# Two orders in a hybrid encoder kernel: the seventh product's jobs of the gate pair in a row, and token sums no longer tied behind operands

## The chip, the cores and the metric

The kernel runs on one core of a Trainium2 chip. The metric is the device time of one execution in microseconds (us). Its engines are called as the profile calls them: PE is TensorE (PEld its weight loads), DVE is VectorE, ACT is ScalarE, POOL is GpSimd and SP is SyncE. SP and POOL issue the transfers of this kernel, each on a queue of its own.

## The reference

Two layers of an encoder trunk over 512 tokens of width 2048, in float32. Each layer normalises its input, projects it once onto the columns of two head groups, and adds the normalised output projection back:

```
h = rmsnorm(x, g_pre)
z = h @ w_in                                   # 2048 x 7184, split into the columns below
gq, gk, gv, gg, ga, aq, ak, av, ag = split_columns(z)
log_a = log_sigmoid(ga @ w_alpha + b_alpha) / 16
o_gla = rmsnorm(gla_chunk_causal(gq, gk, gv, log_a), g_gla) * silu(gg)
o_att = rmsnorm(chunk_band_attention(aq, ak, av, rel_bias), g_att) * silu(ag)
y = concatenate([o_gla, o_att]) @ w_out
return x + rmsnorm(y, g_post)
```

The first group is a gated linear attention with 4 heads and a state that runs over chunks of 64 frames; the second is attention with 8 heads over a band of chunks. `ag` is the attention group's gate, `ga` the 16 columns from which the forget gate is made.

## The kernel before

**Precision.** Every large product is made of float32 numbers that are split into a high and a low part (`split`, L107): ACT casts the high part (`wh` for a weight, L236), DVE subtracts it from the source to get the low part (`wl`, L246), and PE adds three products, high by high, high by low and low by high.

**Fast products.** A projection block is 512 columns wide. Most are taken in pairs, and a pair is computed by `fast_gemm` with the seven products of a Strassen scheme in place of eight: `P1` to `P7` are products of a sum of weight tiles with a sum of token tiles, and each is cut into four chunks `c` of the inner dimension. One such piece is a `Job`. A job's weight comes from a tile of the ring `H` (four buffers of 512 KB), which holds one weight of the pair, is filled for `P1`, and is then added to or subtracted from for `P5`, `P6`, `P7` and `P4`, and of the ring `raw` (five buffers), which brings the second weight of a sum. DVE makes these sums (L230, L232, L252). The token sums `S1` to `S4` (`LEFT` names which product reads which) are made once per layer by `make_sums`, split, and mostly written to DRAM by POOL (L619); SP brings them back into the ring `sa` (four buffers, L215).

**Jobs and look-ahead.** All jobs of both layers stand in one list, `stream`. When PE has taken a job, `ahead` writes the loads of up to five jobs further and the casts and subtractions of up to four. The order in which a pair's jobs come is a line of text: `"10 50 11 ..."` means `P1` chunk 0, `P5` chunk 0, `P1` chunk 1 and so on. From the program so written a scheduler sets the order of the instructions on each engine; each engine then runs its own in that order. `tc.issue_after(x)` tells the scheduler to place an instruction behind `x`.

**First layer.** The attention gate's columns are not computed as a fast pair but as three plain products (`std_gemm`, blocks AG0, AG1 and AG2; AG1 and AG2 are 264 columns wide, with the gate's tail and `ga` in AG2). During AG0 and AG1 `first_operands` makes the token operands, chunk by chunk; the last instruction of each is kept in the list `ends`. The float32 tokens that the sums are made of stand in `full`, and those of the first half, `full[0, c]`, in the four buffers of the ring `H`. During AG1 and AG2 the task `token_sums` makes the 16 sums from them: per chunk two subtractions `S1` and `S3` (`sub`), then `S2` (L631) and `S4` (L634), each followed by its split. After AG2 comes the first fast pair, AV (attention values), whose `H` loads need the buffers of `full[0, c]`.

**Second layer.** Here AG1 and AG2 form a fast pair of their own (`GATE_PAIR`), in the order `PROD_GATE`. Its weights are 264 wide (264 KB a load), its `P4` takes `H` after the weight of `P2` has been added to it (L252) and loads nothing, and its last read of an `H` buffer is `P4`'s. `P2` is collected in two PSUM tiles of its own (`ax` in the profile). After the pair come the QK products (L430, features on the partitions), whose first job, `P1` chunk 0, loads an `H`. At the end of the gate pair ACT also has the Silu of the gates (L784) and loads another table of functions (L62).

Of the kernel before, what the change touches and what calls it, by code (L numbers as in the profile page):

```python
# [11 lines left out]
ALU = mybir.AluOpType  # L12
# [24 lines left out]
def hybrid_trunk(  # L37
# [13 lines left out]
    nc = tc.nc  # L51
# [20 lines left out]
    def slot(tag, shape, dtype=F32):  # L72
        return slots.tile([P] + shape, dtype, tag=tag, name=nm(tag))
# [19 lines left out]
    def dram(shape, name):  # L93
        return dpool.tile(shape, F32, tag=name, name=name)
# [3 lines left out]
    sa_d = [{(n, c): dram([P, 1024], f"{n}{l}{c}") for n in ("S1", "S2", "S3", "S4", "A22") for c in range(4)} for l in range(L)]  # L98
# [5 lines left out]
    def flat(t):  # L104
        return t.bitcast(F32).rearrange("p a b -> p (a b)")
# [30 lines left out]
    def order(text):  # L136
        return [("P" + z[0], int(z[1])) for z in text.split()]
# [3 lines left out]
    PROD_OUT = order("10 20 11 21 12 13 50 51 60 61 22 23 52 53 62 63 30 31 32 33 70 71 72 73 40 41 42 43")  # L141
    PROD_FRONT = order("20 21 22 23 10 11 12 13")
    PROD_REST = order("50 51 52 53 60 61 30 62 63 31 70 32 71 72 73 33 40 41 42 43")
    PROD_GATE = order("10 50 11 51 12 52 13 53 60 30 61 31 62 32 63 33 70 20 71 21 72 22 73 23 40 41 42 43")
    GATE_PAIR = (AG1, AG2)
    LEFT = {"P5": "S1", "P6": "S2", "P3": "S4", "P7": "S3", "P4": "A22"}
    SPARE = ("g12", "g13", "g16", "g17")
# [107 lines left out]
    for l in range(L):  # L255
        if l:
# [5 lines left out]
            pr = {}  # L262
            stream += [Job(l, k, c, *GATE_PAIR, pr) for k, c in PROD_GATE]
        else:
# [277 lines left out]
    full = {}  # L542
# [57 lines left out]
            A[kh, half, c] = op  # L600
            yield

    def make_sums(dst, tags, parts, home={}, behind=None):
        stage = [0]

        def sub(c, out, a, b):
            with tc.issue_after(behind(c)) if behind and c else nullcontext():
                nc.vector.tensor_tensor(out=out, in0=a, in1=b, op=ALU.subtract)

        def put(name, c, src):  # L610
            if (name, c) in home:
                op = A[name, c] = slot(home[name, c], [2, 512], F32R)
            else:
                tag = tags[stage[0] % len(tags)]
                op = rtile(tag, dtype=F32R) if tag == "H" else slot(tag, [2, 512], F32R)
                stage[0] += 1
            with tc.issue_after(last_cast[0]):
                split(op[:, 0, :], op[:, 1, :], src)
            nc.gpsimd.dma_start(dst[name, c], flat(op))  # L619
            written.add((id(dst), name, c))  # L620

        for c in range(4):
            a11, a12, a21, a22 = parts(c)
            yield
            sub(c, a22, a21, a22)
            put("S1", c, a22)
            yield
            sub(c, a21, a11, a21)
            put("S3", c, a21)
            yield  # L630
            nc.vector.tensor_tensor(out=a22, in0=a22, in1=a11, op=ALU.subtract)  # L631
            put("S2", c, a22)
            yield
            nc.vector.tensor_tensor(out=a12, in0=a12, in1=a22, op=ALU.add)  # L634
            put("S4", c, a12)
            yield

    def token_sums(l):
        tags, home = (("g10", "g16", "H"), HOMES) if l else (STAGE, HOME)
        return make_sums(sa_d[l], tags, lambda c: (full[0, c][:, 0, :], full[0, c][:, 1, :], full[1, c][:, 0, :], full[1, c][:, 1, :]), home, None if l else lambda c: ends[-3 if c == 1 else -1])  # L640

    VT = ("g16", "g17", "g4", "g5", "g6", "g7", "g12", "g13")
    V, U = {}, {}
# [55 lines left out]
            nc.tensor.matmul(ps[:, t * P : (t + 1) * P], ones, dg[:, t, :], start=True, stop=True)  # L699
        nc.scalar.copy(rb, ps)  # L700

    ends = []

    def first_operands():
        for ch in CO:
            kh, c = divmod(ch, 4)
            while ch not in U:
                yield
            for half in range(2):
                if kh == 0:  # L710
                    full[half, c] = rtile("H") if half == 0 else slot(KEEP[c], [2, 512])
                dst = full[half, c][:, kh, :]
                tok = slice(half * 256, (half + 1) * 256)
                with tc.issue_after(ends[-2]) if len(ends) >= 2 else nullcontext():
                    for kk in range(2):
                        nc.vector.scalar_tensor_tensor(
                            out=dst[:, kk * 256 : (kk + 1) * 256], in0=V[ch][:, kk, tok],
                            scalar=gcol[:, 2 * ch + kk : 2 * ch + kk + 1], in1=rb[:, tok], op0=ALU.mult, op1=ALU.mult,
                        )
                if half == 0:  # L720
                    op = slot(f"a1{kh + 1}{c}", [2, 512], F32R)
                elif kh == 0:
                    op = slot(A21[c], [2, 512], F32R)
                else:
                    while cursor[0] < NCH:
                        yield
                    op = rtile("sa", (2, 512), F32R)
                ends.append(split(op[:, 0, :], op[:, 1, :], dst))
                if half and kh:
                    nc.gpsimd.dma_start(sa_d[0]["A22", c], flat(op))  # L730
                A[kh, half, c] = op
                yield
        yield from load_forget_gate(0)
# [43 lines left out]
    def layer(l):  # L777
# [136 lines left out]
        if l:  # L914
# [8 lines left out]
            drain()  # L923
            fast_gemm(l, GATE_PAIR, gate_consume, prod=PROD_GATE)
            tasks.append(load_forget_gate(l))
# [662 lines left out]
```

## Time and profile before

| | us |
|---|---|
| runs (3) | 1615.96, 1617.78, 1618.01; median 1617.78 |
| the profiled execution | 1617.69 |
| its span, from the first to the last instruction | 1615.9 |
| PE busy in it | 1595.7 |
| DVE, ACT, POOL busy | 1279.2, 920.6, 134.9 |
| moved by DMA | 441.39 MB, mean 273 GB/s |

In the profile's rows a group or an instruction is named by its line, engine and operation, and by the tiles it writes and reads, without buffer numbers. In brackets or behind a bar stands how long its engine was idle before it and what ended that. PEclk, or the granted clock, is the share of its full speed that PE's clock had. `q1` is SP's queue of transfers and `q0` POOL's. `SPq` rows are SP issuing a transfer; the transfer itself lands later.

### The profile page before, as it was taken

Reading aid. Unit: us, or ns where it says so; the run is one execution under the profiler, and the core shown is the slowest. Engines: PE = TensorE matmul, PEld = TensorE weight load, DVE = VectorE, ACT = ScalarE, POOL = GpSimd, SP = SyncE. Lnnn points to the kernel's source line nnn. Section 1 sums busy time; section 2 is a strip of 40 time slices with the busy share of each in tenths; the row PEclk is TensorE's granted clock in tenths of the full one; section 3 lists DMA queues with packets and bytes.
Section 4 is the critical chain, followed back from the end, with each engine's and each line's share of the span. In section 5 each row is a group of like instructions: output and inputs, shape, how many; then the busy total and the mean of one; then the engine's idle time right before and its main releaser. Section 6 shows DMA issues by size and latency. Waiting matters only on the chain.

```text
span 1615.9 us, 25135 instructions
## 1 busy us (share of the span) xinstructions
PE 1595.7 (99%) x9158; PEld 1377.2 (85%) x9158; DVE 1279.2 (79%) x1697; ACT 920.6 (57%) x1535; POOL 134.9 (8%) x206
## 2 busy tenths in 40 slices
PE   9989999999999999999999998999999999999998
PEld 7978999998888777888888898999988877788886
DVE  5977868678677877998989877785886878689887
ACT  7545445657455556664786445456575545565654
POOL 0220000000000010100122000000000100101001
PEclk9999999999999999999999999999999999999999
DMA  9797777685767768689889987857858687686887
GB/s 349 234 402 249 260 263 245 215 295 184 269 222 272 273 216 312 223 303 401 299 267 357 364 285 264 308 199 239 312 203 285 216 290 250 218 306 241 330 304 202
DMA packets 137229, 441.39 MB, mean 273 GB/s; under 512 B 14885, under 2 KB 27429, under 8 KB 137073
## 3 DMA queue, kind: packets, MB, share of 16 engines
q1 hardware_dynamic: 119952, 377.86, 66.7%
q0 software_dynamic: 16864, 61.63, 10.9%
q8 instruction: 72, 1.18, 0.3%
q14 instruction: 53, 0.43, 0.1%
q10 hardware_dynamic: 288, 0.30, 0.1%
HBM read 380.20 MB, written 61.62 MB: 273 GB/s over the span
## 4 chain that ended last, share of the span: by engine, by line
PE 87%; DMA 4%; issue 4%; DVE 3%; ACT 1%; POOL 1%; POOLq 0%; SPq 0%; DVEq 0%; ACTq 0%
PE mm L440 51%; PE mm L430 19%; PE mm L353 5%; PE ax L440 3%; PE ax L1009 2%; DMA H<-in_w_dram 2%; DMA raw<-in_w_dram 2%; PE ax L1195 1%; DVE wl L246 1%; PE ax L992 1%; PE ax L1167 1%; PE ax L972 1%; PE ax L971 1%; PE ax L970 1%; DMA S<-g 0%
## 5 line engine op out<-in xcount | busy, mean ns | idle before, releaser
L440 PE MATMUL mm<-wh,sa 128*128 128x512 f32 (+1 forms) x1600 | 510.3, 390 | 1.7 <-DMA sa<-S 1.1
L236 ACT CAST wh<-H 128x1024 fp32r<-128x1024 f32 (+1 forms) x256 | 261.4, 1024 | 213.5 <-PE mm L440 81.7
L246 DVE TENSOR_TENSOR wl<-H,wh 128x1024 fp32r<-128x1024 f32 (+1 forms) x256 | 303.4, 1188 | 92.1 <-PE mm L440 29.4
L440 PEld LDWEIGHTS mm<-wh,sa 128*128 128x128 f32 x1600 | 297.7, 188 | 71.3 <-issue 7.7
L236 ACT CAST wh<-raw 128x1024 fp32r<-128x1024 f32 (+2 forms) x237 | 236.2, 1002 | 202.4 <-PE mm L440 78.2
L246 DVE TENSOR_TENSOR wl<-raw,wh 128x1024 fp32r<-128x1024 f32 (+2 forms) x237 | 272.7, 1154 | 59.8 <-PE mm L440 23.9
L440 PE MATMUL mm<-wl,sa 128*128 128x512 f32 (+1 forms) x800 | 309.3, 387 | 0.0
L430 PE MATMUL mm<-sa,wh 128*128 128x256 f32 x1280 | 237.7, 285 | 0.0
L440 PE MATMUL mm<-wh,a 128*128 128x512 f32 (+1 forms) x672 | 219.1, 391 | 4.1 <-ACT wh L236 4.1
L430 PEld LDWEIGHTS mm<-sa,wh 128*128 128x128 f32 x1280 | 200.4, 191 | 0.4
L430 PE MATMUL mm<-sa,wl 128*128 128x256 f32 x640 | 181.1, 283 | 0.2 <-DVE wl L246 0.2
L440 PEld LDWEIGHTS mm<-wl,sa 128*128 128x128 f32 x800 | 150.3, 188 | 29.2 <-DVE wl L246 0.9
L230 DVE TENSOR_TENSOR H<-H,raw 128x1024 f32<-128x1024 f32 (+1 forms) x144 | 170.1, 1188 | 0.9
L440 PEld LDWEIGHTS mm<-wh,a 128*128 128x128 f32 x672 | 125.1, 189 | 30.0 <-ACT wh L236 5.0
L440 PE MATMUL mm<-wl,a 128*128 128x512 f32 (+1 forms) x336 | 130.8, 390 | 0.0
L430 PEld LDWEIGHTS mm<-sa,wl 128*128 128x128 f32 x640 | 122.4, 191 | 0.5 <-DVE wl L246 0.5
L440 PE MATMUL mm<-wh,g 128*128 128x512 f32 (+1 forms) x416 | 120.5, 368 | 0.5 <-ACT wh L236 0.4
L484 POOL TENSOR_TENSOR sm<-sm,mhalf 128x2 f32<-128x2 f32 (+2 forms) x40 | 50.7, 1267 | 696.6 <-DVE sm L1019 389.4
L232 DVE TENSOR_TENSOR raw<-H,raw 128x1024 f32<-128x1024 f32 (+1 forms) x56 | 66.4, 1186 | 49.7 <-DMA raw<-in_w_dram 45.9
L430 PE MATMUL mm<-a,wh 128*128 128x256 f32 x512 | 96.1, 288 | 3.9 <-ACT wh L236 3.9
L390 ACT COPY ev<-mm 128x512 f32<-128x512 f32 (+1 forms) x112 | 64.2, 573 | 54.8 <-PE mm L440 39.2
L252 DVE TENSOR_TENSOR H<-H,raw 128x1024 f32<-128x1024 f32 (+1 forms) x48 | 56.6, 1180 | 43.8 <-DMA raw<-in_w_dram 42.9
(273 smaller groups left out, 2414.5 us busy)
## 6 DMA issues: line engine op xcount, KB each, us to landing
raw<-in_w_dram SPq DMA_DIRECT2D x287, 512.0 KB, 5.2
sa<-S SPq DMA_DIRECT2D x188, 512.0 KB, 4.4
H<-in_w_dram SPq DMA_DIRECT2D x60, 512.0 KB, 5.6
sa<-A SPq DMA_DIRECT2D x48, 512.0 KB, 5.8
sa<-oS SPq DMA_DIRECT2D x32, 512.0 KB, 5.6
S<-g POOLq DMA_DIRECT2D x30, 512.0 KB, 8.0
raw<-in_w_ag_dram SPq DMA_DIRECT2D x32, 264.0 KB, 4.3
oS<-g POOLq DMA_DIRECT2D x16, 512.0 KB, 4.6
```

Of the source, the lines that this page charges most:

```text
L230: nc.vector.tensor_tensor(out=h, in0=h, in1=r, op=ALU.add)
L232: nc.vector.tensor_tensor(out=r, in0=h, in1=r, op=ALU.subtract)
L236: last_cast[0] = nc.scalar.copy(self.wh[:, z, :], src[:, z, :]).ins
L246: last_low[0] = nc.vector.tensor_tensor(out=self.wl[:, z, :], in0=self.src[:, z, :], in1=self.wh[:, z, :].bitcast(F32), op=ALU.subtract).ins
L252: nc.vector.tensor_tensor(out=h, in0=h, in1=self.src, op=ALU.add)
L353: nc.tensor.matmul(pss[o], a(part, kk, o) if callable(a) else a[:, part, t], rhs[:, kk, :], start=(i == 0 and kk == 0 and m == 0), stop=(i ...
L390: last_copy[0] = nc.scalar.copy(e, src[t]).ins
L430: nc.tensor.matmul(dst, lhs[:, kk, f], a[:, part, tok], start=(fresh and kk == 0 and m == 0 and ft % 2 == 0), stop=(c == 3 and kk == 1 and ...
L440: last_mm[0] = nc.tensor.matmul(out_ps[t], a[:, part, tok], rhs[:, kk, :], start=(fresh and kk == 0 and m == 0), stop=(c == 3 and kk == 1 ...
L484: nc.gpsimd.tensor_tensor(out=out_r, in0=v, in1=mhalf[:, : v.shape[-1]], op=ALU.pow)
L970: nc.tensor.matmul(ps[:, :n], self.qh[:, t], self.kh[:, :n], start=True, stop=False)
L1009: nc.tensor.matmul(o, self.pt[i][:, j * P : (j + 1) * P], av[hd // 4, j // 2][:, j % 2, (hd % 4) * P : (hd % 4 + 1) * P], start=(j == 0), ...
```

## The change

Two things are changed. In the second layer's gate pair the seventh product's four jobs come in a row, and then the second and the last product alternate, chunk by chunk; before, the seventh and the second alternated, and the last product's four jobs came at the end. And in the first layer the subtractions for `S1` and `S3` of chunks 1 to 3 are no longer tied behind the splits that end the operands; what is left of the diff takes the argument for that tie away.

```diff
-    PROD_GATE = order("10 50 11 51 12 52 13 53 60 30 61 31 62 32 63 33 70 20 71 21 72 22 73 23 40 41 42 43")
+    PROD_GATE = order("10 50 11 51 12 52 13 53 60 30 61 31 62 32 63 33 70 71 72 73 20 40 21 41 22 42 23 43")
...
-    def make_sums(dst, tags, parts, home={}, behind=None):
+    def make_sums(dst, tags, parts, home={}):
         stage = [0]
 
-        def sub(c, out, a, b):
-            with tc.issue_after(behind(c)) if behind and c else nullcontext():
-                nc.vector.tensor_tensor(out=out, in0=a, in1=b, op=ALU.subtract)
+        def sub(out, a, b):
+            nc.vector.tensor_tensor(out=out, in0=a, in1=b, op=ALU.subtract)
...
-            sub(c, a22, a21, a22)
+            sub(a22, a21, a22)
             put("S1", c, a22)
             yield
-            sub(c, a21, a11, a21)
+            sub(a21, a11, a21)
             put("S3", c, a21)
...
-        return make_sums(sa_d[l], tags, lambda c: (full[0, c][:, 0, :], full[0, c][:, 1, :], full[1, c][:, 0, :], full[1, c][:, 1, :]), home, None if l else lambda c: ends[-3 if c == 1 else -1])
+        return make_sums(sa_d[l], tags, lambda c: (full[0, c][:, 0, :], full[0, c][:, 1, :], full[1, c][:, 0, :], full[1, c][:, 1, :]), home)
...
-    ends = []
-
     def first_operands():
+        ends = []
```

What the scheduler makes of it is seen on the queues. On SP, between the last loads of AG2 and the first products of AV in the first layer, `H_1154`, `H_1184`, `H_1291` and `H_1325` are the four `H` loads of AV, `raw_1064` to `raw_1124` the last weights of AG2, the other `raw` the second weights of AV, and `sa` its token sums. The transfers in the order before:

```order
L172 DMA H_1154<-in_w_dram 128x1024
L215 DMA sa_1383<-S_86 128x1024
L172 DMA raw_1214<-in_w_dram 128x1024
L172 DMA raw_1295<-in_w_dram 128x1024
L172 DMA raw_1343<-in_w_dram 128x1024
L172 DMA H_1184<-in_w_dram 128x1024
L172 DMA raw_1362<-in_w_dram 128x1024
L172 DMA raw_1381<-in_w_dram 128x1024
L172 DMA H_1291<-in_w_dram 128x1024
L172 DMA raw_1411<-in_w_dram 128x1024
L215 DMA sa_1413<-S_87 128x1024
L215 DMA sa_1432<-S_94 128x1024
```

Behind these comes `H_1325`. In the change the same place reads:

```order
L164 DMA raw_1124<-in_w_ag_dram 128x528
L172 DMA H_1184<-in_w_dram 128x1024
L215 DMA sa_1383<-S_86 128x1024
L172 DMA raw_1214<-in_w_dram 128x1024
L172 DMA raw_1295<-in_w_dram 128x1024
L172 DMA raw_1343<-in_w_dram 128x1024
L172 DMA H_1291<-in_w_dram 128x1024
L172 DMA raw_1362<-in_w_dram 128x1024
L172 DMA raw_1381<-in_w_dram 128x1024
L172 DMA H_1325<-in_w_dram 128x1024
L215 DMA sa_1413<-S_87 128x1024
L215 DMA sa_1432<-S_94 128x1024
```

`H_1154` has moved ahead of AG2's last weight, `H_1184` past four transfers, `H_1291` past two loads counted from the first `H`, and `H_1325` past the three that now stand behind it. On DVE, a little earlier in the same stage, `a_127` and `a_130` are token operands of the first half, `wl` the low parts of AG1's and AG2's weights, and the `g` and `H` tiles those of the sums. Before:

```order
L246 TENSOR_TENSOR wl_864<-raw_776,wh_816 128x528
L109 TENSOR_TENSOR g_129_752<-g_128_749,g_129_752 128x512
L716 SCALAR_TENSOR_TENSOR g_128_749<-g_76_432,gcol,bias_178 128x256 x2
L608 TENSOR_TENSOR g_110_643<-g_110_643 128x512
L631 TENSOR_TENSOR g_67_383<-g_67_383,H_339 128x512
L246 TENSOR_TENSOR wl_909<-raw_818,wh_866 128x528
L109 TENSOR_TENSOR a_130_763<-H_737,a_130_763 128x512
```

In the change (line numbers behind the edit are one or two lower):

```order
L607 TENSOR_TENSOR g_119_696<-g_119_696 128x512
L109 TENSOR_TENSOR g_148_888<-g_110_643,g_148_888 128x512
L630 TENSOR_TENSOR g_67_383<-g_67_383,H_339 128x512
L109 TENSOR_TENSOR g_129_752<-g_128_749,g_129_752 128x512
L714 SCALAR_TENSOR_TENSOR g_128_749<-g_76_432,gcol,bias_178 128x256 x2
L246 TENSOR_TENSOR wl_909<-raw_818,wh_866 128x528
L607 TENSOR_TENSOR g_119_696<-H_684,g_119_696 128x512
L109 TENSOR_TENSOR a_130_763<-H_737,a_130_763 128x512
```

Counted over the whole queue, four instructions of the sums more stand ahead of `a_130_763`: three of those above (`g_119_696` twice, `g_148_888`) and the second subtraction of chunk 1. On SP in the second layer, between the gate pair's last loads and the QK pair, `H_9826` is the first `H` of QK, `H_9852` (`H_9844` in the change) its second. Before:

```order
L164 DMA raw_9725<-in_w_ag_dram 128x528
L215 DMA sa_9872<-S_102 128x1024
L172 DMA raw_9870<-in_w_dram 128x1024
L172 DMA raw_9909<-in_w_dram 128x1024
L215 DMA sa_9911<-S_103 128x1024
L172 DMA raw_9997<-in_w_dram 128x1024
L172 DMA raw_10039<-in_w_dram 128x1024
L215 DMA sa_9999<-S_104 128x1024
L172 DMA raw_10072<-in_w_dram 128x1024
L172 DMA H_9826<-in_w_dram 128x1024
L215 DMA sa_10041<-S_105 128x1024
L172 DMA H_9852<-in_w_dram 128x1024
```

In the change:

```order
L164 DMA raw_9791<-in_w_ag_dram 128x528
L215 DMA sa_9864<-S_102 128x1024
L215 DMA sa_9911<-S_103 128x1024
L172 DMA raw_9862<-in_w_dram 128x1024
L172 DMA raw_9909<-in_w_dram 128x1024
L215 DMA sa_9999<-S_104 128x1024
L172 DMA H_9826<-in_w_dram 128x1024
L215 DMA sa_10041<-S_105 128x1024
L172 DMA raw_9997<-in_w_dram 128x1024
L172 DMA H_9844<-in_w_dram 128x1024
L172 DMA raw_10039<-in_w_dram 128x1024
L172 DMA H_9883<-in_w_dram 128x1024
```

The first `H` has moved up past three loads; the second stands as many transfers behind the last gate weight as the first did, and behind it loads and `H` alternate. On all engines the order differs at these two places alone, from the tail of AG1 to the middle of AV in the first layer and from the gate pair's last third into the QK pair in the second.

## The prediction

> **What bounds the kernel now.** I read the page's first rows, then the waits of TensorE (PE), its timeline at the longest of them, the chain of waits there, and last the clock.
>
> ```profile
> span 1615.9 us, 25135 instructions
> PE 1595.7 (99%) x9158; PEld 1377.2 (85%) x9158; DVE 1279.2 (79%) x1697; ACT 920.6 (57%) x1535; POOL 134.9 (8%) x206
> ```
>
> PE is busy all but 20 us of the span. No instruction is added or removed on it by this change, so it can only win or lose idle time and clock. The waits of PE over the whole span, and behind them the one row that the stretch 60 to 124 us gives for the same wait:
>
> ```profile
> PE mm L440 <- ACT wh L236: 5.1, 6, 3.3
> PE mm L430 <- ACT wh L236: 3.9, 1, 3.9
> ...
> PE mm L440 <- ACT wh L236: 4.5, 4, 3.3
> ```
>
> Two places hold most of it. In PE's timeline (start, duration, what ran, and in brackets the idle time before it):
>
> ```profile
> 73.77 0.39 PE L353 MATMUL mm<-wh,a 128*128 128x264 f32 x1 [0.64 <-ACT t L784]
> ...
> 108.17 0.73 PE L440 MATMUL mm<-wh,a 128*128 128x512 f32 x2 [0.81 <-ACT wh L236]
> ...
> 114.01 0.39 PE L440 MATMUL mm<-wh,g 128*128 128x512 f32 x1
> 117.70 0.73 PE L440 MATMUL mm<-wh,a 128*128 128x512 f32 x2 [3.30 <-ACT wh L236]
> ...
> 976.72 0.28 PE L440 MATMUL mm<-wh,g 128*128 128x264 f32 x1
> 980.91 0.74 PE L430 MATMUL mm<-a,wh 128*128 128x256 f32 x4 [3.92 <-ACT wh L236]
> 982.17 0.58 PE L430 MATMUL mm<-a,wl 128*128 128x256 f32 x1 [0.52 <-DVE wl L246]
> ```
>
> Place A is the start of the first layer's AV pair, place B the start of the second layer's first QK pair. At both, PE waits for the high part `wh` of a weight that stands in a tile `H`, and ACT, which casts it, waits for the load. The chain of waits says so:
>
> ```profile
> 98.52 17.98 DMA H<-in_w_dram
> 118.65 63.98 PE mm L440 x274
> ...
> 969.17 10.56 DMA H<-in_w_dram
> ```
>
> Behind each stall the clock is down. Columns: the stretch, its length, busy time (and count) of PE, PEld, DVE, ACT and POOL, granted clock, DMA share, GB/s; the first row has PE alone.
>
> ```profile
> 70.00:80.00 10.00, 9.36 (x77) 1.00 0.84 277
> ...
> 118.60:122.06 3.46, 3.41 (x8) 2.74 (x9) 3.46 (x4) 0.78 (x1) 0.00 (x0) 0.51 0.53 217
> 982.00:985.60 3.60, 3.43 (x16) 3.43 (x17) 2.86 (x4) 2.59 (x3) 0.00 (x0) 0.53 1.01 396
> ```
>
> So each of the two costs its idle time and about 3.46 x 0.49 = 1.7 us (3.60 x 0.47 = 1.7 us) of lost clock. A: 4.5 + 1.7 = 6.2 us. B: 3.92 + 0.52 + 1.7 = 6.1 us. Together 12.3 us is the most that this change can win there. Around the 0.64 us wait the clock stays at 1.00, so I cost a stall near 1 us at its own length. The Trainium skill (TensorE: Matmul & The Clock Gate, Part 1: The HAM clock gate) gives the half clock after an idle window of about 3.4 us and the full one after a busy window as long. The length agrees; the idle time before 117.70 was only 3.30 us, so going by the page A would have kept its clock, and 1.7 us less would be there to win.
>
> **Place A: the token sums untied.** The four `H` buffers hold the first layer's token chunks until that chunk's last sum is split, and only then can SP load AV weights into them. Untied, the sums stand earlier on DVE, so the loads stand earlier on SP. The fourth `H` had three 512 KB transfers (0.524 MB) ahead of it that now come behind it, and the third had two more loads ahead (the order pieces show both). How fast SP's queue moved between 88 and 118 us, beside POOL's writes of the sums, and the issues at the fourth `H`:
>
> ```profile
> q1 hardware_dynamic: 1785, 6.51, 53.1%
> q0 software_dynamic: 1707, 5.99, 49.1%
> ...
> 90.86 0.78 SPq L172 DMA_DIRECT2D H<-in_w_dram  x1
> 95.38 0.33 SPq L172 DMA_DIRECT2D raw<-in_w_dram  x1
> 95.81 2.52 SPq L215 DMA_DIRECT2D sa<-S  x2
> 98.52 1.08 SPq L172 DMA_DIRECT2D H<-in_w_dram  x1
> ...
> 116.60 1.99 ACT L236 CAST wh<-H 128x1024 fp32r<-128x1024 f32 x2 [7.54 <-DMA H<-in_w_dram]
> ```
>
> SP's queue (q1) got 6.51 MB / 30 us = 0.217 MB/us. Three transfers fewer are 3 x 0.524 / 0.217 = 7.2 us: the load lands at 109.3 instead of 116.5, its cast (1.0 us) ends at 110.3. PE came to the end of its earlier work at 114.4, of which 1.0 us were waits of the same kind (0.81 and, of the 0.4 left of 4.5, one of two). Without those it is there at 113.4. The stall goes, with 3 us in hand. If the whole 12.5 MB of both queues were SP's rate (0.417), the gain in landing is 3.8 us and the cast ends at 113.7, a stall of 0.3 us at most. Two transfers fewer take the wait for the third `H` away on both bounds (4.8 or 2.5 us against 0.8). The Trainium skill (DMA: Bandwidth & Descriptors, Queues, rings and completion order) has each DMA engine go round-robin between queues with work; the two rows, 53% and 49%, agree, and by that rule it is the 7.2 us. What comes late next are the three transfers put back (landing near 116.5). They feed the pair's sixth and third products, three jobs after the fourth `H` is used. A job there is 12 matmuls, 2.8 us by the chain's 63.98 for 274; 8.4 us less an addition and a cast leaves over 5.
>
> The price is on DVE. Ahead of the low part of the last operand of chunk 3 (`a`) stand four more 512-wide sum instructions.
>
> ```profile
> 56.58 0.71 DVE L246 TENSOR_TENSOR wl<-raw,wh 128x528 fp32r<-128x528 f32 x1 [0.37 <-ACT a L108]
> ...
> 70.65 0.69 DVE L109 TENSOR_TENSOR a<-H,a 128x512 fp32r<-128x512 f32 x1
> 71.25 0.68 DVE L608 TENSOR_TENSOR g<-H,g 128x512 f32<-128x512 f32 x1
> ...
> 72.00 0.40 PE L353 MATMUL mm<-wh,a 128*128 128x264 f32 x2
> ```
>
> Start to start one takes 0.60 us, four 2.4. The first of them falls into the 0.37 us in which DVE idled. The low part is then done at 71.34 + 2.4 - 0.37 = 73.37, and PE reads it at 72.00: 1.4 us of stall. The 0.64 us wait behind it, for the eviction of that product, comes later by the same and shrinks a little, since ACT had two casts in front of the eviction and now has had time for them: minus 0.2. I take 1.2 us; bounds 0 (PE finds other matmuls in the new order) and 2.4 (nothing is covered). Place A then wins 6.2 - 1.2 = 5.0 us.
>
> **Place B: the gate pair's order.** Same weights, same operands, same matmuls. The fourth product reads `H` last, and it now stands at jobs 22, 24, 26 and 28 of 28 instead of 25 to 28, so the first `H` frees three jobs earlier, the second two, the third one. In SP's order the first `H` of the QK pair moves up past three 512 KB loads, and the second takes the very place where the first stood. The queue between 966 and 980 us, the cast and what ACT does around it:
>
> ```profile
> q1 hardware_dynamic: 1364, 4.97, 90.2%
> q0 software_dynamic: 221, 0.59, 10.6%
> ...
> 972.14 0.76 ACT L784 ACTIVATE t<-ev 128x264 f32<-128x264 f32 x2 [0.16 <-DVE ev L395]
> ...
> 977.12 0.67 ACT L784 ACTIVATE t<-mm 128x264 f32<-128x264 f32 x2
> 977.81 1.28 ACT L62 ACT_TABLE_LOAD   x1
> 979.82 1.04 ACT L236 CAST wh<-H 128x1024 fp32r<-128x1024 f32 x1 [0.72 <-DMA H<-in_w_dram]
> ...
> 251.30 2.88 PE mm L430 x24
> ```
>
> At 4.97 MB / 14 us = 0.355 MB/us three transfers are 4.4 us: the first `H` lands at 979.7 - 4.4 = 975.3, its cast ends at 976.4, before PE is through the gates at 977.0. With POOL's bytes counted in (0.397) it is 4.0 us and 976.8, just in time. The second `H` lands where the first did, at 979.7, is cast by 980.8 and wanted when the first QK job (24 matmuls, 2.9 us) ends at 979.9. That leaves a stall of 1.0 us. ACT says the same from its side: two more Silus of the second product (0.76 us) and the table load now stand behind the first cast, and 977.12 + 0.67 + 0.76 + 1.28 + 1.04 is 980.9. Lower bound 0.2 (the second `H` gains from the operands that are fetched sooner), upper 1.6 (it gains nothing and the low part on DVE adds its 0.52 again). The third and fourth `H` come 2 transfers later each, 3 us, while PE has two jobs, 5.8 us, between them. B wins 6.1 - 1.0 = 5.1 us.
>
> The seventh product's row needs four operands and four weights in a row. The last of its operands is issued at the same place of SP's order as before:
>
> ```profile
> 958.66 0.38 SPq L215 DMA_DIRECT2D sa<-S  x1
> ...
> DMA to landing us min/median/max: 3.7/3.7/3.7
> ...
> 958.81 1.70 PE mm L440 x14
> 962.22 1.22 PE mm L440 x10
> ```
>
> The three operand loads issued between 954 and 960 landed after 3.7 us each, so this one is there at 962.4. A gate job is 12 matmuls of 0.122 us, 1.46; the seventh product begins near 959.0 (the last two rows are of the chain, and the 14 matmuls are that job with two of the one before), its fourth job at 959.0 + 3 x 1.46 = 963.4. It is covered by 1.0 us, and I cost it at nothing; uncovered it is the slower rival below. A fourth-product job needs the addition of the weight that the job before it has just used; in the new order that addition stands on DVE ahead of the low part of that job, so nothing waits for it that did not before.
>
> **Sum.** The profiled execution took 1617.69 us, of which 1.8 lie outside the span, and the median of the runs is 1617.78. 1617.7 - 5.0 - 5.1 = **1607.6 us**, 0.6% less. With all costs at their low bound it is 1617.7 - 6.2 - 5.9 = 1605.6, with all at their high bound 1617.7 - 3.5 - 4.5 = 1609.7.
>
> **Rivals.**
> - *One place pays, the other keeps its stall.* At A, if POOL's writes, which also start earlier, take more than half of the engines; at B, if the 0.2 to 0.6 us in hand for the first `H` are not there and the stall stays near 3 us with its clock. For it: at B the margin is thin. Against: A has 3 us. 1617.7 - 5.1 = 1612.6 us.
> - *The change doesn't do what its order says.* SP issues in order, so an `H` that is free early still waits behind a load whose buffer isn't: the fourth `H` at A stands behind the last two `raw` loads. For it: in the profile they went out just ahead of the third `H`. Against: that was 90.9 us, 7.6 ahead of 98.52. Only DVE's 1.2 us and small gains are left: 1617 to 1619 us.
> - *Bytes decide, not their order: slower.* The seventh product's row takes 4 x (0.524 + 0.270) = 3.2 MB in four jobs; at 0.355 MB/us that is 8.9 us against 5.9 of PE, a stall of 3.0, and every byte fetched for it keeps the QK loads where they were, so that B's 6.1 us stay; by the same rule A keeps its own and adds 1.2. 1617.7 + 3.0 + 1.2 = 1621.9 us. It decides once that operand takes over 4.7 us to land (963.4 - 958.66); the row says 3.7.
>
> **Chances.** The forecast 0.77, one place alone 0.13, nothing moves 0.05, slower 0.05. A difference under 0.2% (3.2 us) can't be told from none here. Faster: the first two cases less a little, 0.89; same 0.06; slower 0.05. The range reaches from just under the low bounds to the one-place case: 1605 to 1613 us.
>
> **What would show it.** Right: no wait of 3 us on `wh<-H` in PE's waits, no stretch of half clock near 119 and 983 us, a wait of 1 to 2 us near 72 us in place of 0.6, and about 1 us near 980 us less what A has won. The fourth `H` of A issued near 91 us instead of 98.5. Wrong: idle time on L430 with the clock at 0.5, an operand `sa` in PE's waits among the gates, or PE waiting for `wl` or `a` for over 2.5 us between 66 and 82 us.

## The result, and the profile after

| | before | change |
|---|---|---|
| runs, us | 1615.96 to 1618.01 (4) | 1605.49, 1605.61, 1606.90, 1608.99 |
| median, us | 1617.30 | 1606.26 |
| the profiled execution, us | 1617.69 | 1608.99 |

The ratio is 0.9936 (95% interval 0.9919 to 0.9953): 11.0 us less at the medians, and the forecast of 1607.6 lies 1.3 us beside the measured median. Two repeats on other occasions gave 0.9936 (0.9925 to 0.9948) and 0.9929 (0.9917 to 0.9941). The profiled execution of the change is the slowest of its four. It took 8.7 us less than that of before.

The page's first rows of the change, and its waits of PE over the whole span (us in all, times, longest):

```profile
span 1607.2 us, 25131 instructions
PE 1592.8 (99%) x9158; PEld 1376.8 (86%) x9158; DVE 1278.0 (80%) x1697; ACT 920.5 (57%) x1535; POOL 134.2 (8%) x206
...
PE mm L430 <- ACT wh L236: 1.6, 2, 1.4
PE mm L353 <- DVE sa L114: 1.5, 1, 1.5
...
PE mm L440 <- ACT wh L236: 0.5, 2, 0.3
PE mm L353 <- DVE a L109: 0.4, 1, 0.4
...
PE mm L353 <- ACT t L782: 0.3, 1, 0.3
```

PE's idle time, span less busy, went from 20.2 to 14.4 us. The waits of 5.1 us on L440 and 3.9 us on L430 have become 0.5 and 1.6. The 1.5 us on L353 lie at 6.8 us, at the start of the program, where the change alters nothing; the two repeats don't have them in their profiles.

**Place A** has no stall and no half clock any more. The chain of waits shows the fourth `H`, the timeline of SP the issues around it, that of ACT its cast; the last row is the stretch 110 to 120 us with PE busy 9.86 us at a clock of 1.00 (before: 6.49 us).

```profile
95.49 17.21 DMA H<-in_w_dram
...
85.62 5.22 SPq L172 DMA_DIRECT2D raw<-in_w_dram  x3
90.94 1.65 SPq L172 DMA_DIRECT2D H<-in_w_dram  x1
92.68 2.72 SPq L172 DMA_DIRECT2D raw<-in_w_dram  x2
95.49 1.28 SPq L172 DMA_DIRECT2D H<-in_w_dram  x1
...
112.81 2.00 ACT L236 CAST wh<-H 128x1024 fp32r<-128x1024 f32 x2 [1.43 <-DMA H<-in_w_dram]
...
110.00:120.00 10.00, 9.86 (x44) 7.83 (x43) 7.19 (x9) 5.40 (x7) 0.59 (x1) 1.00 1.03 418
```

The third `H` went out when it did before (90.9 us), the fourth 3.0 us earlier (before 98.52). It landed at 112.7 us, before at 116.5.

**Place B** is not gone but smaller. ACT's timeline, then PE's:

```profile
970.06 1.05 ACT L236 CAST wh<-H 128x1024 fp32r<-128x1024 f32 x1 [1.74 <-DMA H<-in_w_dram]
972.75 0.77 ACT L782 ACTIVATE t<-ev 128x264 f32<-128x264 f32 x2 [1.63 <-DVE ev L395]
973.42 0.65 ACT L782 ACTIVATE t<-mm 128x264 f32<-128x264 f32 x2
974.09 1.28 ACT L62 ACT_TABLE_LOAD   x1
975.38 1.99 ACT L236 CAST wh<-H 128x1024 fp32r<-128x1024 f32 x2
...
971.84 0.63 PE L430 MATMUL mm<-a,wh 128*128 128x256 f32 x4
...
976.48 0.74 PE L430 MATMUL mm<-a,wh 128*128 128x256 f32 x4 [1.40 <-ACT wh L236]
977.43 1.17 PE L430 MATMUL mm<-sa,wh 128*128 128x256 f32 x4 [0.21 <-ACT wh L236]
```

The first QK job starts at 971.84 without a wait. The second waits 1.40 us for the cast of the second `H`, and that cast waits for no transfer: it starts the moment the table load ends, and stands there behind four Silus.

Where the time went is best seen not by the idle rows but by the matmuls themselves, since both kernels run the same 9158 of them. The table gives how much earlier the matmul of the same number starts than in the profiled execution of before (us; worked out from the starts of each trace). A loss is a fall from one column to the next, a gain a rise. Inside the gate pair, between 950 and 1010 us, matmuls of one number belong to other jobs, at both ends of that stretch they don't. Later sections use the other rows.

```
matmul that before starts at    60     105    130    600    950    1010   1300   1600
change                        -0.69  -1.54   5.37   6.01   5.27   7.60   7.43   8.33
change, first repeat           0.14  -0.95   6.31   5.48   5.75   9.03   9.01  10.79
change, second repeat          0.12  -1.60   5.08   5.45   5.29   9.09   9.12  10.91
e1 sums only                   0.04  -0.96   6.40   6.68   5.95   5.55   5.58   6.49
e2 gate order only            -0.42  -0.43  -0.24  -0.90  -0.21   3.33   3.35   4.42
e3 last product at the end     0.12  -0.86   6.49   7.35   7.60   7.65   7.65   9.48
e4 later table load           -0.08  -1.38   5.98   5.46   5.96  10.88  10.91  12.72
e6 chunk 1 untied             -0.91  -0.45   5.99   6.32   6.52  11.86  10.67  12.35
e7 chunks 2, 3 untied         -0.03  -0.79  -1.03  -1.56  -1.74   3.22   1.76   3.55
e8 last product early         -0.22  -1.48   5.82   2.47   2.35   9.33   9.35  10.23
e9 three rows                 -0.47  -1.33   6.03   5.52   5.09  10.00   8.62  10.14
e10 later table load again    -0.84  -1.68   5.50   3.79   3.75   8.82   8.84  10.65
```

Between 60 and 130 us the change and its repeats win 6.1, 6.2 and 5.0 us, between 950 and 1010 us 2.3, 3.3 and 3.8 us. The 0.9 to 1.8 us between 1300 and 1600 us stand in every kernel, also in e1 and e2, which share no edit, so I don't count them to either place. They arise around a wait for an operand at 1328 us, which is 1.15 us long in the profile of before, 0.5 to 0.7 us in four of the others and not there in the rest. Whether other executions of before have it as long, the one profile of before doesn't show.

### The profile page after: what moved, and what is told of

Read it like the earlier page. It is cut to its first block, busy times and chain, and to the rows that moved or that the text cites. A ratio compares the mean times of both kernels' runs of the same rounds, so it can differ in the third digit from the quotient of the medians.

```text
span 1607.2 us, 25131 instructions
## 1 busy us (share of the span) xinstructions
PE 1592.8 (99%) x9158; PEld 1376.8 (86%) x9158; DVE 1278.0 (80%) x1697; ACT 920.5 (57%) x1535; POOL 134.2 (8%) x206
## 4 chain that ended last, share of the span: by engine, by line
PE 88%; issue 4%; DMA 3%; DVE 3%; ACT 1%; POOL 1%; POOLq 0%; SPq 0%; ACTq 0%; DVEq 0%
PE mm L440 51%; PE mm L430 20%; PE mm L353 5%; PE ax L440 3%; PE ax L1007 2%; DMA H<-in_w_dram 2%; PE ax L1193 1%; PE ax L990 1%; PE ax L1165 1%; DVE wl L246 1%; PE ax L970 1%; PE ax L969 1%; PE ax L968 1%; DMA S<-g 1%; ACT wh L236 0%
## 5 line engine op out<-in xcount | busy, mean ns | idle before, releaser
L440 PE MATMUL mm<-wh,sa 128*128 128x512 f32 (+1 forms) x1600 | 510.1, 390 | 1.2 <-DMA sa<-S 0.6
L246 DVE TENSOR_TENSOR wl<-H,wh 128x1024 fp32r<-128x1024 f32 (+1 forms) x256 | 303.4, 1188 | 92.8 <-PE mm L440 28.1
L440 PEld LDWEIGHTS mm<-wh,sa 128*128 128x128 f32 x1600 | 297.6, 188 | 70.6 <-issue 8.1
L246 DVE TENSOR_TENSOR wl<-raw,wh 128x1024 fp32r<-128x1024 f32 (+2 forms) x237 | 272.9, 1154 | 59.2 <-PE mm L440 24.6
L440 PE MATMUL mm<-wl,sa 128*128 128x512 f32 (+1 forms) x800 | 309.2, 387 | 0.0
L430 PE MATMUL mm<-sa,wh 128*128 128x256 f32 x1280 | 238.1, 285 | 0.2 <-ACT wh L236 0.2
L440 PE MATMUL mm<-wh,a 128*128 128x512 f32 (+1 forms) x672 | 218.2, 389 | 0.0
L430 PEld LDWEIGHTS mm<-sa,wh 128*128 128x128 f32 x1280 | 200.6, 192 | 0.9 <-ACT wh L236 0.4
L430 PE MATMUL mm<-sa,wl 128*128 128x256 f32 x640 | 180.8, 283 | 0.0
L440 PEld LDWEIGHTS mm<-wl,sa 128*128 128x128 f32 x800 | 150.3, 188 | 28.8 <-DVE wl L246 0.4
L440 PEld LDWEIGHTS mm<-wh,a 128*128 128x128 f32 x672 | 124.8, 188 | 25.1
L440 PE MATMUL mm<-wl,a 128*128 128x512 f32 (+1 forms) x336 | 130.2, 388 | 0.0
L430 PEld LDWEIGHTS mm<-sa,wl 128*128 128x128 f32 x640 | 122.2, 191 | 0.2 <-DVE wl L246 0.2
L440 PE MATMUL mm<-wh,g 128*128 128x512 f32 (+1 forms) x416 | 120.3, 367 | 0.2
L430 PE MATMUL mm<-a,wh 128*128 128x256 f32 x512 | 95.7, 287 | 1.4 <-ACT wh L236 1.4
L252 DVE TENSOR_TENSOR H<-H,raw 128x1024 f32<-128x1024 f32 (+1 forms) x48 | 56.6, 1180 | 43.0 <-DMA raw<-in_w_dram 40.7
```

The lines of the kernel that those rows point to most:

```text
L246: last_low[0] = nc.vector.tensor_tensor(out=self.wl[:, z, :], in0=self.src[:, z, :], in1=self.wh[:, z, :].bitcast(F32), op=ALU.subtract).ins
L252: nc.vector.tensor_tensor(out=h, in0=h, in1=self.src, op=ALU.add)
L430: nc.tensor.matmul(dst, lhs[:, kk, f], a[:, part, tok], start=(fresh and kk == 0 and m == 0 and ft % 2 == 0), stop=(c == 3 and kk == 1 and ...
L440: last_mm[0] = nc.tensor.matmul(out_ps[t], a[:, part, tok], rhs[:, kk, :], start=(fresh and kk == 0 and m == 0), stop=(c == 3 and kk == 1 ...
```

## The experiments

### Each part alone

e1 is the change with the old order of the gate jobs; e2 is the kernel before with the new one.

```diff
 e1, against the change:
-    PROD_GATE = order("... 70 71 72 73 20 40 21 41 22 42 23 43")
+    PROD_GATE = order("... 70 20 71 21 72 22 73 23 40 41 42 43")
 e2, against before:
-    PROD_GATE = order("... 70 20 71 21 72 22 73 23 40 41 42 43")
+    PROD_GATE = order("... 70 71 72 73 20 40 21 41 22 42 23 43")
```

> The changed kernel with the old order of the gate jobs: of the change only the untied token sums are left. If the two places are independent and the untied sums are what removes the stall near 119 us (idle 4.5 us in all there, and 1.7 us of half clock), the second layer's stall near 980 us stays as it was: 1617.3 - 6.1 = 1611.2 us, 1610 to 1612.5; no wait of 3 us on wh<-H near 117 us, one of 3 to 4 us near 980 us, one stretch of half clock. Rival (the stall at 119 us has to do with the gates' order or only moved): 1616 to 1618 us.

> The kernel before with the new order of the gate jobs alone. If that order frees the first H buffer early enough, the wait near 980 us goes from 3.9 + 0.5 us with 1.7 of half clock to 1.6 us, with half clock in some executions: 1617.3 - 2.8 to 1617.3 - 4.5, so 1612.8 to 1614.5 us, 1612.4 if the effects of the two parts add up to that of the change; the stall of 3.3 us near 117 us stays. Rival (the seventh product's four operands in a row starve PE, which the changed kernel hides by having won time before): 1616 us and more, with a wait on sa among the gates.

Measured: e1 1609.74 us (1608.28 to 1612.03), ratio 0.9949 (0.9936 to 0.9963). e2 1612.75 us (1611.30 to 1615.65), ratio 0.9969 (0.9957 to 0.9980). Both medians lie just under the ranges expected. Before on the same chip: 1617.58. The waits of PE in e1 over the span, and in e2 between 100 and 125 us and between 940 and 1000 us:

```profile
PE mm L430 <- ACT wh L236: 3.9, 1, 3.9
```

```profile
PE mm L440 <- ACT wh L236: 4.3, 4, 3.4
...
PE mm L430 <- ACT wh L236: 1.4, 2, 1.1
```

Each part cures its own place and leaves the other as it was, so neither rival stands. The gains at the medians are 7.8 and 4.8 us, the sum 12.7 against some 11 for the change; the intervals (6.0 to 10.4 and 3.2 to 7.0 us) are too wide to say that the two parts cost each other anything.

### Which part of the new gate order helps

e3 keeps the seventh product's row but puts the last product back to the end.

```diff
-    PROD_GATE = order("... 70 71 72 73 20 40 21 41 22 42 23 43")
+    PROD_GATE = order("... 70 71 72 73 20 21 22 23 40 41 42 43")
```

> The changed kernel, but with the last product's four jobs in a row at the end: the seventh product's row stays, the second and the last product don't alternate. If B's gain comes from the last product's jobs that end earlier and so free their weights and raw buffers and let the H loads be issued ahead of three others, the stall near 980 us is back: 1610.5 to 1612.5 us, first H landing near 979 us. Rival (the gain comes from the seventh product's row, whose operands are fetched sooner): 1605.5 to 1607.5 us, as the change.

Measured: 1612.07 us (1608.04 to 1615.09), ratio 0.9964 (0.9950 to 0.9979). The profiled execution is the fastest of the seven. Waits of PE between 940 and 1000 us, and the first `H` in the chain of waits:

```profile
PE mm L430 <- ACT wh L236: 4.7, 1, 4.7
PE mm L430 <- DVE wl L246: 0.4, 1, 0.4
...
961.64 10.82 DMA H<-in_w_dram
```

The stall is back and longer than in before (3.92 + 0.52). The row of the seventh product alone wins nothing at B (7.60 to 7.65 in the table); it is the last product's alternation with the second that matters. By SP's timeline five second weights go out ahead of the first `H` here, as in before; in the change two. This `H` lands at 972.5 us, in an execution that leads by 8.0 us; in before it is 979.7.

e8 keeps the alternation without the row, e9 three rows with the last product's ahead of the second's.

```diff
-    PROD_GATE = order("... 70 71 72 73 20 40 21 41 22 42 23 43")
 e8:
+    PROD_GATE = order("... 70 40 71 41 72 42 73 43 20 21 22 23")
 e9:
+    PROD_GATE = order("... 70 71 72 73 40 41 42 43 20 21 22 23")
```

> The changed kernel with the alternation but without the row: seventh and last product alternate, the second product's four jobs come at the end. The last product's jobs then end four jobs earlier than in the change, three H loads are issued ahead of the last gate operands, and the casts of the first two H stand ahead of the Silus and the table load on ACT. If early H loads are the cause of B's gain, the first and second H cost no wait at all: 1603 to 1605 us. Rival (the bytes decide, not their order: the weights and operands of the second product, now behind H, come late): a wait of 2 to 4 us on raw or sa among the last gates, 1607 to 1610 us.

> The changed kernel with the seventh, the last and the second product's gate jobs in three rows, in this order. The last product ends four jobs before the gates do, so all four H loads of the first QK pair are issued together and early, and the casts stand ahead of the second product's Silus and the table load. No part of the sum is mixed here. If early H loads are the cause of B's gain: no wait on wh<-H near 975 us, a lead of 6 to 7 us gained between 960 and 1010 us, 1603 to 1605 us. Rival (the last product's four operands and weights in a row behind those of the seventh starve PE): a wait of 2 us or more on sa or raw among the gates, 1606 to 1610 us.

In both, the last product's weights lack the second product's, which is added to `H` in the second product's job (L252 of before), and in e8 the read-out of the seventh product holds three jobs of the last one too. So the expectation of e9 was wrong in saying that nothing is mixed. The instructions and bytes are as many, but a last-product job waits for one addition less, and the times are read with that in mind. Measured: e8 1606.44 us (1604.07 to 1607.93), ratio 0.9929 (0.9916 to 0.9941); e9 1606.30 us (1604.40 to 1608.37), ratio 0.9928 (0.9915 to 0.9940); I had expected 1603 to 1605 us for both. In neither does PE wait for a QK `wh` between 940 and 1000 us. e9's longest wait there, in PE's timeline, is on an operand:

```profile
959.28 0.36 PE L440 MATMUL mm<-wh,sa 128*128 128x264 f32 x1 [1.43 <-DMA sa<-S]
```

At B e8 wins 7.0 us and e9 4.9 (table), so early `H` loads do take the whole stall away. In e9 part of that is paid back by the operand that comes late behind so many rows: the rival, that the operands and weights in a row starve PE, is real at this size. e8's median is no lower than the change's. Its profiled execution loses 3.4 us between 130 and 600 us, at a wait on DVE at L995 (2.1 us) with half clock behind it; its fastest executions, at 1604.1 us, lie about as much below it and may be without that loss. Neither is a version to use, since their gates are others.

### Which of the ties mattered

e6 and e7 stand on e4 (below), whose B has little noise. e6 ties the sums of chunks 2 and 3 again, e7 those of chunk 1.

```diff
+            with tc.issue_after(behind(c)) if behind and c in TIED else nullcontext():
+                nc.vector.tensor_tensor(out=out, in0=a, in1=b, op=ALU.subtract)
 e6: TIED = (2, 3)      e7: TIED = (1,)
```

> The changed kernel with the later table load, and the token sums of chunks 2 and 3 tied again as before; only chunk 1's are untied. SP then issues one H load early instead of two, and the fourth H of the first layer one 512 KB transfer later than in the change, two earlier than before. If H's place in that order is what ended the stall near 117 us, the fourth H lands about 2.4 us later than in the change, where it had no margin: a wait of 0.5 to 2.5 us on wh<-H, with or without half clock, against 0.3 to 0.6 us less delay near 72 us: 1604.3 + 0.2 to + 3.5, so 1604.5 to 1608 us. Rival (any untied sum does, since DVE is then ahead): no wait near 117 us and 1603.5 to 1604.2 us.

> The changed kernel with the later table load, and the token sums of chunk 1 tied again as before; only those of chunks 2 and 3 are untied. Two H loads go early as in the change, but the fourth has as many transfers ahead of it as before. If the transfers ahead of the fourth H decide, its wait of about 3 us near 117 us and the half clock are back: 1604.3 + 4.5 to + 7, so 1609 to 1611.5 us. Rival (two early H are enough): 1603.5 to 1605.5 us.

Measured beside before at 1618.00: e6 1604.65 us (1603.85 to 1604.83), ratio 0.9921 (0.9908 to 0.9934); e7 1614.35 us (1611.44 to 1618.68), ratio 0.9983 (0.9973 to 0.9994). The fourth `H` in the chain of waits and PE's waits in 100 to 125 us, of e6:

```profile
95.00 17.09 DMA H<-in_w_dram
...
PE mm L440 <- ACT wh L236: 0.2, 1, 0.2
```

and of e7, the longest of its waits from PE's timeline:

```profile
100.01 17.47 DMA H<-in_w_dram
...
118.67 0.73 PE L440 MATMUL mm<-wh,a 128*128 128x512 f32 x2 [3.62 <-ACT wh L236]
```

e7 came out slower than I expected, but as the theory had it: two early `H` loads are not enough, the fourth was issued later than before (100.0 against 98.5 us) and the stall is back. e6 refutes my reason for it. One more transfer stood ahead of the fourth `H` than in the change, and it went out at 95.0 us all the same (change: 95.5). So the number of transfers ahead is not what sets its issue; and the tie that held everything was chunk 1's alone. The sums are made in one sequence, so a tied first subtraction of chunk 1 holds back all that come behind it.

What its issue goes with is DVE's last read of the buffer that the fourth `H` fills, the low part of chunk 3's last sum. In before, the change and e6 it is:

```profile
97.80 0.69 DVE L109 TENSOR_TENSOR g<-H,g 128x512 fp32r<-128x512 f32 x1 [0.17 <-ACT g L108]
...
92.95 0.69 DVE L109 TENSOR_TENSOR g<-H,g 128x512 fp32r<-128x512 f32 x1 [0.96 <-ACT g L108]
...
94.28 0.68 DVE L109 TENSOR_TENSOR g<-H,g 128x512 fp32r<-128x512 f32 x1
```

It ends at 98.49, 93.64 and 94.96 us, in e7 at 99.54; the fourth `H` went out at 98.52, 95.49, 95.00 and 100.01. So in before and in e6 it left the moment its buffer was free, in e7 0.5 us later. In before SP was also busy with the issues ahead until 98.33 us, so there two bounds meet; in e6 the buffer alone decided. Only in the change was it 1.9 us late for its buffer, behind the loads ahead of it.

e6 also doesn't pay for the sums on DVE: from 60 to 105 us it gains 0.5 us, where the change and every other kernel with all sums untied loses 0.8 to 1.7. That is one profile, and e6's whole time isn't told apart from e4's, so I take it as likely, not shown.

### What is left at B

e4 moves the second layer's table load from directly behind the gates to behind the first QK pair's `P5` chunk 0.

```diff
-            act_table("natural_log_exp_and_others")
...
+        def table_late(k, c):
+            if l and (k, c) == ("P5", 0):
+                act_table("natural_log_exp_and_others")
+
-        fast_gemm(l, PAIRS[1], qk_consume(0), rate=2.1, feature_major=True)
+        fast_gemm(l, PAIRS[1], qk_consume(0), rate=2.1, feature_major=True, after=table_late)
```

> The changed kernel, but in the second layer the table load of ACT for the exponential is moved from directly behind the gates' last Silus to behind the first QK pair's fifth product, so that the casts of the second and third H no longer stand behind it (1.28 us). If ACT's order, not the landing of the second H, sets the 1.40 us wait that is left near 975 us, that wait goes to 0.1 to 0.4 us, the 0.21 us wait behind it and its half clock are gone: 1.3 to 3.2 us less than the change, 1603 to 1605 us. Rival (the second H lands no sooner than 975 us, so the cast waits for it instead): 1605.5 to 1607 us, with the cast's wait ended by the DMA.

Measured: 1604.27 us (1603.62 to 1607.69), ratio 0.9920 (0.9906 to 0.9935). ACT's timeline, and PE's waits between 940 and 1000 us:

```profile
973.60 2.00 ACT L236 CAST wh<-H 128x1024 fp32r<-128x1024 f32 x2 [0.41 <-DMA H<-in_w_dram]
```

```profile
PE mm L430 <- ACT wh L236: 0.7, 2, 0.5
PE mm L430 <- DVE wl L246: 0.5, 1, 0.5
```

So ACT's order did set the wait. The cast now starts 1.8 us earlier (0.7 of it is the lead that this execution already had at 950 us), and only 0.41 us later than ACT could, with the transfer as the next bound; PE's wait for it falls from 1.40 to 0.5 us, not to the 0.1 to 0.4 that I expected. At B 4.9 us are won against 2.3 to 3.8 in the change, but not all of that is the table load's: up to 976 us of before, still among the gates, e4 gains 0.5 us and the change and its repeats lose 0.3 to 0.7. From there to 1010 us e4 wins 4.4 us, the change and its repeats 2.6, 4.0 and 4.4.

To see whether this is a better version, I ran it beside the change.

> The change itself once more, on the same chip and in the same rounds as the three kernels beside it: 1605.5 to 1607.5 us. The wait of 1.2 to 1.6 us near 975 us has half clock behind it in some executions and none in others, so single times fall into two groups some 1.7 us apart; with it in all executions they would lie within 1 us.

> The changed kernel with the later table load once more, in the same rounds as the change: 1603.5 to 1605 us, 1.5 to 3 us less than the change. If the gain of the first time was the chip's, the two lie within 0.5 us.

> The change, as the partner of the two kernels ahead: 1605.5 to 1607.5 us.

Measured: e5 (with e6 to e8) 1606.81 us (1606.30 to 1608.41); e10 and e11 in the same rounds 1605.24 us (1602.31 to 1610.66) and 1606.14 us (1605.88 to 1607.52), ratios 0.9925 (0.9911 to 0.9940) and 0.9929 (0.9917 to 0.9941). e10 gains 5.1 us at B, about as e4 did (6.1 from 976 us on), but its times scatter by 8 us. In its profile PE waits for no QK `wh` at all; in e4's 0.7 us of such waits are left. Beside the change e10 is 0.9 us faster at the medians, less than the 1.5 to 3 that I expected; that the whole kernel is faster by 1 to 2 us is likely from the medians and is not resolved by the intervals. e5's times don't fall into two groups as I had expected, only one of five lies apart (1608.41).

## Why the prediction was right

**A wins 5.0: measured 5.0 to 6.2, from two terms that were both a little off.** The relief was put at 6.2 us (4.5 idle, 1.7 of clock). From 105 to 130 us the table shows 6.7 to 7.3 us in the change and its repeats. Part of the rest is idle time that the rows don't show: a matmul's row lasts longer than its turn. Two rows of before's timeline, on either side of the 0.64 us wait at 73.77 us:

```profile
72.84 0.28 PE L353 MATMUL mm<-wh,a 128*128 128x264 f32 x1
...
73.99 0.28 PE L353 MATMUL mm<-wl,a 128*128 128x264 f32 x1
```

Without a wait these matmuls start 0.12 us apart and are shown 0.28 us long. Here the next one starts 0.93 us after the first, and the one behind it 0.22 us later: 0.91 us lost in all where the row says 0.64. At A the 512-wide matmuls have a turn of 0.23 us; from the starts at 114.01, 117.70 and 118.03 us 3.56 us are lost where the row says 3.30. So each wait costs about 0.27 us more than it shows, and A's four together 1.1 us, enough for the rest.

The price of the sums on DVE was put at 1.2 us. The waits near 72 us are 0.71 us in the change against 0.64, which reads as no price at all; by the table, 60 to 105 us, it is 0.9, 1.1 and 1.7 us. The same hidden share is the reason: in the change PE stops there three times (0.14, by the starts, 0.41 and 0.30 us), in before once.

**The fourth `H` lands 7.2 us earlier, with 3 us in hand: not so.** It was issued at 95.49, not near 91, and landed 3.8 us earlier with nothing to spare; that is the size of the weaker of the two bounds, but not its reason (a faster queue). The step that failed is "three transfers fewer ahead of it, at the queue's rate". In before the fourth `H` left when its own buffer came free, 0.2 us after the issues ahead of it, and untying moved that by 4.9 us, from 98.49 to 93.64. Of these 1.9 us were lost behind the loads ahead, which were issued later than in before: the first of the five `raw` loads at 85.6 us against 82.1, since ahead of it SP now stood on the second `H`, whose buffer came free at 83.0, and on an `sa` behind that, for which it waited on PE until 85.2 (in before 81.2). From 85.62 us on SP worked without a gap at these loads and the third `H`, 5.22 us at three `raw` and 2.72 us at two, where other rows of SP have 0.33 us for one such issue. The third `H` left at 90.9 us, as in before. That was the place of my second rival, in which the fourth `H` stands behind the last `raw` loads; it was there, in part, and what was left of the lead just sufficed. But its reason, a `raw` buffer that isn't free, was not seen: if the ring's five buffers are taken in turn, each had been read for the last time, by DVE at L246, at least 0.5 us before its load's row begins. Why these issues took so long stays open.

**B wins 5.1: measured 2.3 to 3.8.** Right in it: the first `H` in time (its cast starts at 970.06, PE wants it at 971.84), the last product's early end as the cause (e3, e8), ACT's order as one of the two bounds on the second `H` (e4). The term that was mis-sized is the residual stall of 1.0 us: it was 1.40 + 0.21 in the profiled execution of the change. The sum on ACT's side let the last Silus start 0.12 us behind the gates' last matmul, as in before (977.12 against 977.00). In the change they started 0.75 us behind it (972.75 against 972.00): the first cast, now early, had sent its low part on DVE ahead of the evictions that the Silus read.

```profile
971.14 1.22 DVE L246 TENSOR_TENSOR wl<-H,wh 128x1024 fp32r<-128x1024 f32 x1 [2.09 <-ACT wh L236]
972.29 0.76 DVE L395 TENSOR_TENSOR ev<-ax,ev 128x264 f32<-128x264 f32 x2
```

These 0.6 us are the difference. The stall came out at the upper bound that I gave, 1.6 us, but not for its reason, the second `H`'s transfer. And "a stall near 1 us costs its own length alone" failed in this execution: behind 1.61 us of idle the clock was down for 3.41 us, 1.7 us more. In the two repeats, with 1.6 and 1.5 us, it was not.

**The seventh product's row at nothing: not quite.** PE waits for no `sa` or `raw` among the gates of the change. But it waits for the low part of a second-product weight, which it doesn't in before:

```profile
962.33 0.39 PE L440 MATMUL ax<-wl,a 128*128 128x264 f32 x1 [0.37 <-DVE wl L246]
...
959.70 0.71 DVE L252 TENSOR_TENSOR H<-H,raw 128x528 f32<-128x528 f32 x1 [1.37 <-DMA raw<-in_w_ag_dram]
960.95 0.70 DVE L252 TENSOR_TENSOR H<-H,raw 128x528 f32<-128x528 f32 x1
```

DVE had stood 1.37 us for a gate weight, and two additions came ahead of that low part (961.57 us). So "nothing waits for it that did not before" failed too, by 0.37 us and its hidden share; both repeats have the wait (0.36 and 0.37; e10 has 1.27 us, e4 none), and it fits the 0.3 to 0.7 us that the three lose up to 976 us. e9 shows how near the operands were: with the last product's row directly behind it the wait for one is 1.43 us.

**The sum.** 10.1 us were forecast. From 60 to 130 us and from 950 to 1010 us the change's profile gives 6.06 + 2.33 = 8.4 us, the repeats 9.5 and 8.8 us. That is 0.6 to 1.7 us less than forecast; of the 11.0 us between the medians the two places don't account for the rest, and the profiles have 0.9 to 1.8 us of it near 1328 us, where nothing was forecast. So the total was closer than its parts, which were won 0 to 1.2 us higher at A and 1.3 to 2.8 us lower at B than forecast: that it lies 1.3 us beside the median is partly luck.

## What to carry to other kernels

When a load is to go out earlier in a queue that issues in order, read when its own buffer comes free and what holds each load ahead of it; here the count of transfers ahead gave 7.2 us where 3.8 came. When a stall on a load is cured, look on the casting engine for what stands ahead of the next cast, and on the engines that feed it for what the earlier load has put in front: here 2.6 us of Silus and table load were the next bound, and they began 0.6 us late. And to size a stall, compare the starts of the same-numbered matmuls in two traces, since idle rows leave out what a matmul's modelled end covers.

## What the runs showed of the clock

The half-clock stretches start on a fixed grid of 3.41 us. Cut at that grid, the windows view (PE busy in the first column, clock in the third from the end) gives for A and B of before:

```profile
115.16:118.58 3.42, 0.73 (x2) 0.30 (x2) 0.90 (x1) 1.98 (x2) 0.00 (x0) 1.00 1.03 420
118.58:121.99 3.41, 3.34 (x8) 2.67 (x9) 3.41 (x4) 0.72 (x2) 0.00 (x0) 0.50 0.54 221
...
975.33:978.74 3.41, 1.67 (x14) 1.46 (x13) 1.37 (x2) 2.12 (x4) 0.78 (x2) 1.00 1.01 408
978.74:982.15 3.41, 0.74 (x4) 0.53 (x4) 1.23 (x1) 1.40 (x2) 0.87 (x2) 1.00 1.02 409
982.15:985.56 3.41, 3.39 (x16) 3.39 (x17) 2.70 (x3) 2.55 (x3) 0.00 (x0) 0.50 1.02 397
```

The two starts, 118.58 and 982.15, are 863.57 us apart, 253 times 3.4133. For the change, its second repeat and e1:

```profile
974.11:977.52 3.41, 1.80 (x14) 1.39 (x12) 1.13 (x2) 3.25 (x3) 1.60 (x3) 1.00 1.03 413
977.52:980.93 3.41, 3.41 (x16) 3.41 (x17) 3.41 (x4) 2.39 (x4) 0.00 (x0) 0.50 0.92 368
```

```profile
974.11:977.52 3.41, 1.90 (x15) 1.49 (x13) 1.13 (x2) 3.40 (x4) 1.61 (x3) 1.00 1.03 414
977.52:980.93 3.41, 3.41 (x29) 3.41 (x30) 3.41 (x4) 2.73 (x4) 0.00 (x0) 1.00 0.94 379
```

```profile
970.59:974.00 3.41, 0.26 (x3) 0.05 (x1) 0.68 (x1) 2.73 (x5) 1.65 (x3) 1.00 1.04 399
974.00:977.41 3.41, 2.66 (x10) 2.36 (x11) 2.59 (x3) 1.86 (x3) 0.00 (x0) 0.50 1.03 416
977.41:980.83 3.42, 3.42 (x18) 3.42 (x17) 3.42 (x4) 2.90 (x4) 0.00 (x0) 0.50 0.82 315
```

A window with PE busy for 0.3 or 0.7 us was followed by half clock; one with 1.67 (before) or 1.90 us was not, one with 1.80 us (change) was. So in these profiles the border lies near half a window, and PE's modelled busy time doesn't draw it sharply; what does is open. The same stall of e1 as of before (3.9 us) was followed by two windows of half clock instead of one. Half of PE's busy time in them is 3.0 us instead of 1.7. The first slow window was itself not full (2.66 us, in before 3.39), which is the likely reason. A stall's price in clock therefore depends on how it falls on the grid, which differs from execution to execution, and this may account for some of the scatter of single runs.

The Trainium skill (TensorE: Matmul & The Clock Gate, Part 1: The HAM clock gate) has a window of 3413 ns that runs freely, which these starts bear out. It has the half clock after an idle window; here windows in which PE was busy for 0.3 to 1.8 us were enough, so the prediction's reading of that rule, by which A would have kept its clock, doesn't hold.
